# Batched float32 matmul: late stores gated by half of the last batch but one, and the last quarter of the first x loaded in sixteen transfers of eight partitions

## The chip, the cores and the metric

The kernel runs on one core of one Trainium2 chip. The metric is the device time in microseconds (us) of one execution. The time before was 517.37 us, the median of three runs (517.19 to 517.54).

"The profile" is a page of one profiled execution, and "the trace" is the record behind it: every instruction, every DMA packet with queue, size, start and duration, and every completion signal. PE is the matmul engine, SyncE and GpSimd (SP and POOL in the profile) issue DMA transfers here, and sixteen DMA engines carry them.

## The reference

```python
def setup_inputs():
    batch, m, k, n = 32, 512, 1024, 768
    return {
        "x": np.random.randn(batch, m, k).astype(np.float32),
        "weight": np.random.randn(batch, k, n).astype(np.float32),
    }

def reference(x, weight):
    return np.matmul(x, weight).astype(np.float32)
```

The program reads 64 MiB of x and 96 MiB of weights and writes 48 MiB, with no reuse between batches.

## The kernel before

x and weights are loaded by GpSimd, which casts them to bf16 on the way. Only the x of batch 0 comes in float32 through SyncE, because that queue starts sooner (its first issue begins at 0.74 us, GpSimd's at 1.23). Stores go through GpSimd too, up to the last four; those go through SyncE at the end. Loads run three to four batches ahead of the arithmetic.

```python
CHUNKED = {B - 4: (4, 4), B - 3: (4, 4), B - 2: (4, 4), B - 1: (4, 2, 2)}
AHEAD = 3
LATE = 4
...
def load_x(b):
    xs[b] = x_pool.tile([P, MT, K], BF16, name="x_sb")
    nc.gpsimd.dma_start(out=xs[b], in_=x_view[b])
...
def transpose_first(mt):
    xT = xT_pool.tile([P, JT, P, 2], BF16, name="xT")
    for h in range(2):
        pt = tpsum.tile([P, JT, P], F32, name="pt")
        for i in range(JT):
            nc.tensor.transpose(pt[:, i, :], x_first[:, mt, JT * h + i::KT], ident)
        ...
...
x_first = first_pool.tile([P, MT, K], F32)      # 128 partitions, 16 KB each
nc.sync.dma_start(x_first, x_view[0])
load_w(0)
...
for b in range(B):
    if b + AHEAD + 1 < B:
        load_x(b + AHEAD + 1)
    if b + AHEAD < B:
        load_w(b + AHEAD)
    if 0 < b <= B - LATE:
        nc.gpsimd.dma_start(out=out_view[b - 1], in_=outs[b - 1])
    if b == B - 1:
        for late in (B - 2, *range(B - LATE, B - 2)):
            nc.sync.dma_start(out_view[late], outs[late])
    ...
                if last and mt % 2 == 1:
                    pair = mt // 2
                    evacuate(b, pair, pms[pair])
                    if b == B - 1:
                        cols = slice(pair * N2, (pair + 1) * N2)
                        nc.sync.dma_start(out_view[b, :, cols], outs[b][:, cols])
```

The store of batch 30 (B - 2) is the first of the late ones on SyncE, and the others queue behind it, so it is the gate of them all.

## Time and profile before

| what | value | view |
|---|---|---|
| time, median of three runs | 517.37 us | times |
| span of the profiled run | 515.6 us | page |
| data moved | 218.1 MB, 423 GB/s | page, DMA queues |
| chain of waits | DMA 89%, PE 7% | page, chain |
| PE may start on the last two batches / PE ends | 481.2 / 507.3 us | chain, by time |
| last weights piece: first to last of its 16 signals | 490.82 to 495.91 us | completion signals |
| last store, last signal | 514.26 us | completion signals |

Lines of the page of the kernel before. The PE and DMA lines are tenths of busy time in 40 slices of the span. The q lines are DMA queues with packets, MB and their share of the sixteen engines' time. The DMA/PE line is the chain that ended last, and the last line is the group of transposes of x_first (busy us, mean ns, then the idle time ahead of them and what ended it).

```profile
span 515.6 us, 5976 instructions
...
PE   0999898698797888869978799797798877999793
...
DMA  8999999999999999999999999999999999999996
...
q0 software_dynamic: 13824, 126.88, 96.8%
q1 hardware_dynamic: 864, 8.39, 4.0%
q8 instruction: 20, 0.33, 0.2%
...
HBM read 167.77 MB, written 50.33 MB: 423 GB/s over the span
...
DMA 89%; PE 7%; issue 1%; POOL 1%; DVE 0%; ACT 0%; POOLq 0%
...
L82 PE MATMUL pt<-ident,x_first 128*128 128x128 f32 x32 | 6.0, 350 | 12.2 <-DMA x_first<-in_x_dram 12.2
```

The DMA engines are busy in every slice but the last, and the chain that sets the end is nearly all DMA. q0 is the queue of the GpSimd transfers, q1 that of the SyncE ones.

The windows view of the end of the kernel before (per stretch: us from the start, then its length, busy us of PE, PE's weight loads, DVE, ACT and POOL, the granted clock, the DMA busy share, GB/s):

```profile
490.00:494.00 4.00, 4.00 (x26) 2.44 (x25) 0.69 (x1) 1.76 (x3) 0.00 (x0) 1.00 1.07 320
494.00:496.00 2.00, 1.70 (x13) 1.35 (x12) 1.69 (x3) 0.59 (x1) 0.00 (x0) 1.00 0.72 286
496.00:504.00 8.00, 8.00 (x54) 5.34 (x53) 1.67 (x3) 0.00 (x0) 0.00 (x0) 1.00 1.01 424
504.00:508.00 4.00, 3.27 (x21) 1.73 (x18) 1.38 (x2) 2.30 (x4) 0.00 (x0) 1.00 0.96 404
508.00:512.00 4.00, 0.00 (x0) 0.00 (x0) 0.00 (x0) 0.00 (x0) 0.00 (x0) 1.00 0.85 350
512.00:514.00 2.00, 0.00 (x0) 0.00 (x0) 0.00 (x0) 0.00 (x0) 0.00 (x0) 0.64 0.14 58
```

There is one dip, at 494 to 496 us, where the share is 0.72: engines that have finished their loads wait for the gate. From 508 us on the engines drop out one after another.

The reason is that the engines are not equally far along. Each transfer leaves sixteen completion signals. These are the landing offsets of the last weights piece, in us after the first signal, for the kernel before (worked out from the trace):

```
first 490.82, last 495.91:
0.0 0.1 0.1 0.3 0.3 0.9 1.4 2.0 2.5 2.6 2.6 2.6 2.7 4.2 4.2 5.1
```

The trace does not number the engines. But packets on one engine follow each other, so following each packet's end to the next one's start puts nearly all of them on sixteen chains. Queue 8 carries 20 blocks of instructions of 16 KB. They fall on the same eight chains in a cycle, two or three on each, and on the other eight never. The Trainium skill, "Runtime: NRT & Kernel Launch", Instruction fetch mechanics, says that instructions are refilled in 16 KiB blocks over DMA queues of their own; this trace agrees (20 packets of 16 KB), and shows on which engines the cost falls.

### The profile page before, as it was taken

To read this page: it belongs to the slowest core of one execution; us is meant where nothing else is said; L and a number is where in the kernel's file an instruction comes from. 1 tells how busy PE (TensorE), PEld (TensorE's weight loads), DVE (VectorE), ACT (ScalarE), POOL (GpSimd) and SP (SyncE) were. 2 spreads that over 40 slices of the span, in tenths; PEclk is the share of its full clock that TensorE was granted. 3 is DMA by queue.
4 is the path that set the end of the run, shared out by engine and by line. 5 is a ranking of instruction groups with operands and counts; after the bars stand their busy time and mean duration, and the time that the engine had idled before them with its cause. 6 is when DMAs were issued, how large, how long until landed. Compare 5 with 4: busy or idle time off the path is not lost.

```text
span 515.6 us, 5976 instructions
## 1 busy us (share of the span) xinstructions
PE 429.0 (83%) x2576; PEld 279.2 (54%) x2576; DVE 129.8 (25%) x196; ACT 76.3 (15%) x129; POOL 51.9 (10%) x102
## 2 busy tenths in 40 slices
PE   0999898698797888869978799797798877999793
PEld 0666565465464555546645466464465545665461
DVE  0433232213232312221223232122222313232231
ACT  0011111111011111111111111011110111111011
POOL 3011100011011010100101001100111010111000
PEclk9999899989799988988989999799998989899898
DMA  8999999999999999999999999999999999999996
GB/s 255 218 218 211 218 271 275 256 237 276 277 275 269 231 273 276 274 274 245 251 278 276 274 260 242 272 274 275 269 243 263 277 273 275 247 248 272 274 368 285
DMA packets 14713, 135.64 MB, mean 263 GB/s; under 512 B 1632, under 2 KB 1632, under 8 KB 3040
## 3 DMA queue, kind: packets, MB, share of 16 engines
q0 software_dynamic: 13824, 126.88, 96.8%
q1 hardware_dynamic: 864, 8.39, 4.0%
q8 instruction: 20, 0.33, 0.2%
q14 instruction: 5, 0.04, 0.0%
HBM read 167.77 MB, written 50.33 MB: 423 GB/s over the span
## 4 chain that ended last, share of the span: by engine, by line
DMA 89%; PE 7%; issue 1%; POOL 1%; DVE 0%; ACT 0%; POOLq 0%
DMA w_sb<-in_weight_dram 39%; DMA x_sb<-in_x_dram 25%; DMA out_dram<-out_sb 25%; PE pm L100 7%; PE pt L69 1%; POOL w_sb L61 0%; POOL x_sb L55 0%; ACT out_sb L113 0%; DVE out_sb L112 0%; DVE xT L71 0%; POOL ident masks.py:199 0%; POOL ident masks.py:197 0%; POOLq L132 0%; POOLq L61 0%; POOLq masks.py:199 0%
## 5 line engine op out<-in xcount | busy, mean ns | idle before, releaser
L100 PE MATMUL pm<-w_sb,xT 128*128 128x256 bf16 (+1 forms) x2048 | 374.1, 342 | 66.1 <-DMA w_sb<-in_weight_dram 63.7
L100 PEld LDWEIGHTS <-xT 128*128 128x128 bf16 x2048 | 207.0, 102 | 208.2 <-issue 77.0
L71 DVE COPY xT<-pt 128x1024 bf16<-128x1024 bf16 x124 | 82.9, 689 | 230.6 <-PE pt L69 230.6
L111 ACT COPY out_sb<-pm 128x512 f32<-128x512 f32 x64 | 37.5, 587 | 293.3 <-PE pm L100 293.3
L69 PEld LDWEIGHTS pt<-ident,x_sb 128*128 128x128 f32 x496 | 72.7, 206 | 6.6 <-issue 1.9
L112 DVE COPY out_sb<-pm 128x512 f32<-128x512 f32 x64 | 44.0, 687 | 128.1 <-PE pm L100 128.1
L69 PE MATMUL pt<-ident,x_sb 128*128 128x128 f32 x496 | 75.3, 285 | 0.0
L113 ACT COPY out_sb<-pm 128x512 f32<-128x512 f32 x64 | 37.5, 587 | 137.5 <-PE pm L100 137.4
L55 POOL DMA_DIRECT2D x_sb<-in_x_dram x31 | 16.5, 534 | 176.5 <-DMA w_sb<-in_weight_dram 150.9
L61 POOL DMA_DIRECT2D w_sb<-in_weight_dram x37 | 19.8, 536 | 126.0 <-DMA out_dram<-out_sb 62.8
L132 POOL DMA_DIRECT2D out_dram<-out_sb x28 | 15.1, 538 | 119.0 <-DMA x_sb<-in_x_dram 57.3
L82 PE MATMUL pt<-ident,x_first 128*128 128x128 f32 x32 | 6.0, 350 | 12.2 <-DMA x_first<-in_x_dram 12.2
L82 PEld LDWEIGHTS pt<-ident,x_first 128*128 128x128 f32 x32 | 5.0, 204 | 12.8 <-issue 12.2
L83 DVE CAST xT<-pt 128x512 bf16<-128x512 f32 x8 | 5.6, 728 | 19.2 <-PE pt L82 19.0
L111 ACT ACT_TABLE_LOAD x1 | 1.3, 1283 | 0.7 <-PEq L180 0.7
masks.py:199 POOL TENSOR_SCALAR_AFFINE_SELECT ident<-ident 128x128 f32<-128x128 f32 x1 | 0.3, 289 | 0.1
masks.py:197 POOL MEMSET ident<- 128x128 f32 x1 | 0.2, 224 | 0.0
L180 POOL MEMSET const-float32-0.0<- 128x1 f32 x1 | 0.1, 99 | 0.2 <-issue 0.2
L180 POOL MEMSET const-bfloat16-1.0<- 128x1 bf16 x1 | 0.1, 102 | 0.0
L180 POOL MEMSET const-uint8-127<- 128x1 uint8 x1 | 0.1, 102 | 0.0
L180 POOL MEMSET const-float32-1.0<- 128x1 f32 x1 | 0.1, 99 | 0.0
## 6 DMA issues: line engine op xcount, KB each, us to landing
w_sb<-in_weight_dram POOLq DMA_DIRECT2D x28, 1536.0 KB, 43.2
out_dram<-out_sb POOLq DMA_DIRECT2D x28, 1536.0 KB, 42.0
x_sb<-in_x_dram POOLq DMA_DIRECT2D x31, 1024.0 KB, 39.6
w_sb<-in_weight_dram POOLq DMA_DIRECT2D x7, 768.0 KB, 31.4
out_dram<-out_sb SPq DMA_DIRECT2D x3, 1536.0 KB, 11.4
x_first<-in_x_dram SPq DMA_DIRECT2D x1, 2048.0 KB, 11.3
out_dram<-out_sb SPq DMA_DIRECT2D x2, 768.0 KB, 6.1
w_sb<-in_weight_dram POOLq DMA_DIRECT2D x2, 384.0 KB, 27.5
```

Source lines behind the costliest of these rows:

```text
L55: nc.gpsimd.dma_start(out=xs[b], in_=x_view[b])
L61: nc.gpsimd.dma_start(out=ws[b][:, at:at + n, :], in_=w_view[b, :, at:at + n, :])
L69: nc.tensor.transpose(pt[:, j, :], pairs[:, mt, j::JT], ident)
L71: nc.vector.tensor_copy(xT.rearrange("p j m r -> p (j m r)"), pt.bitcast(BF16).rearrange("p j m -> p (j m)"))
L82: nc.tensor.transpose(pt[:, i, :], x_first[:, mt, JT * h + i::KT], ident)
L83: nc.vector.tensor_copy(xT[:, 2 * h:2 * h + 2].rearrange("p j m r -> p j r m"), pt.rearrange("p (j r) m -> p j r m", r=2),)
L100: nc.tensor.matmul(pm[bank][:, at:at + size], xT[:, ko // 2, :, ko % 2], ws[b][:, ko, off:off + size], start=(ko == 0 and not (together an ...
L111: nc.scalar.copy(o[:, 0:512], pm[0])
L112: nc.vector.tensor_copy(o[:, 512:1024], pm[1])
L113: nc.scalar.copy(o[:, 1024:N2], pm[2])
L132: nc.gpsimd.dma_start(out=out_view[b - 1], in_=outs[b - 1])
L180: nc = _bacc.Bacc("TRN2", target_bir_lowering=False, num_devices=1)
```

## The change

There are two parts. At the start, the last quarter of x_first (partitions x 4 KB) is taken out of the one big transfer and sent in sixteen transfers of eight partitions, meant to load eight DMA engines and to spare the eight others. At the end, the store of batch 30 is cut in halves by columns: the first half, which is evacuated earlier, is the new gate, and the second half goes last. The last piece only gives the slices a common name.

```diff
-        nc.sync.dma_start(x_first, x_view[0])
+        nc.sync.dma_start(x_first[:, :MT - 1], x_view[0, :, :MT - 1])
         load_w(0)
+
+        for half in range(0, P, 32):
+            for at in range(half, half + 4):
+                few = slice(at, half + 32, 4)
+                nc.sync.dma_start(x_first[few, MT - 1], x_view[0, few, MT - 1])
 ...
             if b == B - 1:
-                for late in (B - 2, *range(B - LATE, B - 2)):
+                halves = [slice(pair * N2, (pair + 1) * N2) for pair in range(2)]
+                nc.sync.dma_start(out_view[b - 1, :, halves[0]], outs[b - 1][:, halves[0]])
+                for late in range(B - LATE, B - 2):
                     nc.sync.dma_start(out_view[late], outs[late])
+                nc.sync.dma_start(out_view[b - 1, :, halves[1]], outs[b - 1][:, halves[1]])
 ...
                         if b == B - 1:
-                            cols = slice(pair * N2, (pair + 1) * N2)
-                            nc.sync.dma_start(out_view[b, :, cols], outs[b][:, cols])
+                            nc.sync.dma_start(out_view[b, :, halves[pair]], outs[b][:, halves[pair]])
```

## The prediction

> **What bounds the kernel.** The DMA engines. The page's slices show their mean busy share near 9 tenths throughout; the chain of waits is 89% DMA, PE 7%; HBM moves 218 MB at 423 GB/s. So two things count: the work of each of the sixteen engines, and idle time of the engine that ends last.
>
> **The engines are not equally loaded.** Each transfer leaves sixteen completion signals in the trace. First to last, they are 0.6 us apart for the first weights, 2.3 us at 110 us, 4.0 us at 230 us, 5.1 us from 430 us on. Following packets end to start, I can put them on sixteen engines: the 20 instruction blocks of 16 KB (queue 8, 0.93 us each) fall on the same eight engines in turn, two or three each (1.9 to 2.8 us); the other eight carry none. The Trainium skill, "Runtime: NRT & Kernel Launch", Instruction fetch mechanics, says instructions are refilled in 16 KiB blocks; the trace agrees.
>
> At the end, twelve engines finish the last store by 511.9 us, four at 513.2 to 514.3. Fast ones idle 0.9 to 2.0 us around 494 to 496 (the windows view: DMA share 0.72), because stores on the SyncE queue wait for the whole of batch 30 (495.0); the slowest never idles: its late stores land 3.66 us apart, eight packets of 0.46 us each.
>
> **What the change does.**
> 1. x_first: three quarters over sixteen engines, the last 512 KB on eight. The Trainium skill, "DMA: Bandwidth & Descriptors", How many engines (k), says a SyncE transfer of eight partitions uses the lowest-numbered eight. They get 16 rows of 4 KB in place of 8, the others none. A 16 KB row takes 0.624 us, so 4 KB about 0.156: +1.25 us for eight engines, -1.25 us for eight. I assume that the relieved eight are those with instruction blocks; the order of their first packets leans that way, no proof.
> 2. Sixteen small issues, each taking turns with weight packets of 0.93 us: the last quarter should land at 20 to 24 us; its first use was at 22.8. PE may stall up to 2 us in batch 0; free, since transfers are queued some 40 us ahead.
> 3. Gate: the first half of batch 30 is evacuated at 492.5 us, 2.5 us before the whole. That fills idle time of engines which do not end last: about 0 alone. Rows of 6 KB cost 0.236 us against 0.461 for 12 KB, nothing lost.
>
> **On the critical path.** The slowest engine loses 1.25 us at the start and never idles, so its later landings move up by 1.25 us. Weights that release PE at 481.2 us come earlier too, so PE's end (507.3 us) moves up; from there a last half store needs about 3.5 us, so PE does not bind. 517.37 - 1.25 = 516.1 us. Range 515.4 to 517.2. Faster by over 2%: 0.01; within 2%: 0.98; slower: 0.01.
>
> **What would show it.** Spread of the signals late in the run down from 5.1 to about 2.6 us, with an early spread up to about 2.5 us; span 514.4 us; the dip at 494 to 496 us gone; hardware-queue packets of 4 KB near 0.16 us; the last quarter landing at 20 to 24 us, PE idle at most 2 us in batch 0.
>
> **What would make it wrong.** If the instruction blocks sit on the lowest eight, the skew grows to 7.6 us and the time rises to about 518.6 us. If 4 KB packets cost much more than 0.16 us, the filled engines become the last. If batch 0 stalls for long, the queue could run dry. If the earlier stores hold up the weights of batch 31 on the slow engine, PE ends later and gain is lost.

## The result, and the profile after

The changed kernel took 517.19 us (median of six runs, 516.93 to 518.73), the kernel before in the same rounds 517.45 us (six runs, 516.89 to 517.77). The ratio is 1.0000, with a 95% interval of 0.9987 to 1.0014. Here and below a ratio is the mean time of one kernel's fast runs over the mean of the other's of the same rounds, so it is not quite the ratio of the medians quoted. The forecast gain of 1.25 us is not there: the interval allows at most 0.7 us. In the profile the span is the same too.

Lines of the page after, answering to those of before:

```profile
span 515.6 us, 5998 instructions
...
PE   0039999999999889769978799788798796998793
...
DMA  8999999999999999999999999999999999999996
...
q1 hardware_dynamic: 1264, 8.39, 4.1%
q8 instruction: 20, 0.33, 0.2%
...
DMA 70%; PE 25%; DVE 2%; issue 1%; ACT 0%; POOLq 0%
...
L82 PE MATMUL pt<-ident,x_first 128*128 128x128 f32 x32 | 6.0, 349 | 34.1 <-DMA x_first<-in_x_dram 34.1
```

PE starts batch 0 at 34.1 us instead of 12.2 us, then works without gaps for about ten slices until it has caught up. That is also why the chain now counts 25% for PE: while PE catches up, the chain can be followed through it. The DMA line is the same.

The timeline of the first 36 us after (start, length, engine, line, operation, count):

```profile
0.74 0.39 SPq L117 DMA_DIRECT2D x_first<-in_x_dram  x1
1.19 20.85 SPq L123 DMA_DIRECT2D x_first<-in_x_dram  x16
...
34.05 2.39 PE L82 MATMUL pt<-ident,x_first 128*128 128x128 f32 x9 [34.05 <-DMA x_first<-in_x_dram]
```

The waits view of SyncE's queue after (what its line waited for: us in total, times, longest us):

```profile
SPq L123 <- DMA x_first<-in_x_dram: 10.3, 9, 4.1
```

The sixteen issues take from 1.2 to 22 us: each is 0.62 us long, and nine of them wait 10.3 us in all for earlier transfers. The last of their signals arrive at 33.2 to 34.0 us, and only then does PE start, although its first transposes read the three quarters that had landed by 10.1 us.

The windows view of the end after:

```profile
490.00:494.00 4.00, 4.00 (x28) 2.44 (x26) 0.69 (x1) 1.76 (x3) 0.00 (x0) 1.00 1.07 324
494.00:496.00 2.00, 1.70 (x14) 1.36 (x12) 1.82 (x3) 0.59 (x1) 0.00 (x0) 1.00 0.99 392
496.00:504.00 8.00, 8.00 (x54) 5.30 (x52) 1.54 (x3) 0.00 (x0) 0.00 (x0) 1.00 1.02 430
504.00:508.00 4.00, 3.14 (x19) 1.66 (x17) 1.38 (x2) 2.30 (x4) 0.00 (x0) 1.00 0.81 339
508.00:512.00 4.00, 0.00 (x0) 0.00 (x0) 0.00 (x0) 0.00 (x0) 0.00 (x0) 0.65 0.84 343
512.00:514.00 2.00, 0.00 (x0) 0.00 (x0) 0.00 (x0) 0.00 (x0) 0.00 (x0) 0.50 0.10 43
```

The dip at 494 to 496 us is filled (0.72 to 0.99), and comes back at 504 to 508 us (0.96 to 0.81): the fast engines finish the earlier stores sooner and then wait for PE's last halves. The chain by time says that PE's end hardly moved. Before, then after (start, length, what):

```profile
450.05 31.16 DMA w_sb<-in_weight_dram
...
481.35 2.26 PE pm L100 x8
...
507.31 0.59 ACT out_sb L113
```

```profile
450.58 30.50 DMA w_sb<-in_weight_dram
...
481.21 2.08 PE pm L100 x8
...
507.18 0.59 ACT out_sb L113
```

The weights that release PE land at 481.08 us instead of 481.21, and the last evacuation starts 0.13 us earlier. The forecast said 1.25.

What about the engines? The last weights piece now lands from 489.90 to 495.78 us, so the spread of its signals is 5.9 us, not the forecast 2.6. The next table adds up the time of each chain up to its 700th data packet on the software queue, the same amount of bulk work for every engine. "hw" is the time of data packets on the SyncE queue, "blocks" that of instruction blocks, "stalled" the time by which packets of the software queue took longer than the median for their size. The rest (start, bulk packets, overlap) is nearly the same for all, 458.4 to 459.6 us on the chains that end last.

```
                                        reached at        hw         blocks       stalled
before  no blocks (seven of eight)      465.4 to 466.8    5.4-6.2    0            0.4 to 1.5
        two blocks (six)                468.0 to 468.3    5.8-6.0    1.9          1.0 to 1.4
        three blocks                    470.53            5.96       2.68         3.00
        three blocks                    469.60            5.69       2.68         2.38
after   no blocks, relieved (two)       464.5 to 464.6    4.1-4.5    0            0.4 to 0.6
        two blocks, relieved (six)      466.7 to 467.1    4.6-5.1    1.9          0.7 to 0.9
        no blocks, filled (five)        466.9 to 467.3    7.1-8.0    0            0.4 to 0.6
        three blocks, filled            470.39            7.77       2.68         0.99
        three blocks, filled            470.18            7.93       2.68         1.09
```

(One chain of each kernel is left out: it also carries two 8 KB instruction packets of another queue; it is at 467.0 before and at 468.4 after. The links between packets are inferred. A second linking holds each engine to its eight data packets of every large transfer. It gives the same points and blocks, but for the last two chains after it gives 7.39 and 7.57 us of hw and 1.39 and 1.09 of stalls. So the points are firm, and the split between hw and stalls is good to about 0.4 us.)

Two things stand out. Six of the eight engines with blocks were relieved, and gained 1.3 us; but the two with three blocks before the end, which end last, are among the filled eight. And although those two now carry about 2 us more (1.5 to 1.9 in the second linking), the later of them comes no later than before (470.39 against 470.53): their stalls are 1.3 to 2.0 us shorter (1.3 to 1.6 in the second linking).

### The profile page after: what moved, and what is told of

Same layout as the page of the kernel before. It is cut to its first block, busy times and chain, and to the rows that moved or that the text cites. A ratio compares the mean times of both kernels' runs of the same rounds, so it can differ in the third digit from the quotient of the medians.

```text
span 515.6 us, 5998 instructions
## 1 busy us (share of the span) xinstructions
PE 422.0 (82%) x2576; PEld 276.9 (54%) x2576; DVE 129.8 (25%) x196; ACT 76.3 (15%) x129; POOL 51.9 (10%) x102
## 4 chain that ended last, share of the span: by engine, by line
DMA 70%; PE 25%; DVE 2%; issue 1%; ACT 0%; POOLq 0%
DMA w_sb<-in_weight_dram 31%; DMA out_dram<-out_sb 24%; PE pm L100 22%; DMA x_sb<-in_x_dram 8%; DMA x_first<-in_x_dram 6%; PE pt L69 2%; DVE xT L71 1%; PE pt L82 1%; DVE out_sb L112 1%; ACT out_sb L113 0%; POOLq L61 0%; POOLq L137 0%; POOLq L55 0%
## 5 line engine op out<-in xcount | busy, mean ns | idle before, releaser
L100 PE MATMUL pm<-w_sb,xT 128*128 128x256 bf16 (+1 forms) x2048 | 367.1, 337 | 51.1 <-DMA w_sb<-in_weight_dram 47.4
L100 PEld LDWEIGHTS <-xT 128*128 128x128 bf16 x2048 | 204.5, 101 | 188.8 <-issue 54.6
L82 PE MATMUL pt<-ident,x_first 128*128 128x128 f32 x32 | 6.0, 349 | 34.1 <-DMA x_first<-in_x_dram 34.1
```

Of the source, the lines that this page charges most:

```text
L100: nc.tensor.matmul(pm[bank][:, at:at + size], xT[:, ko // 2, :, ko % 2], ws[b][:, ko, off:off + size], start=(ko == 0 and not (together an ...
```

## The experiments

The theory after the first look at the trace was: the filled eight include two of the block engines, so the engine that ends last gets more work and not less; something else hides the extra. The rivals: the gate or the split undoes a gain of the other; PE's late start costs what the relief gives; the placing of the blocks is drawn anew in each run, so that the two traces can't be compared. The quoted expectations name these theories in their own words or by letters.

### Half of the change: the gate alone

```diff
             if b == B - 1:
-                for late in (B - 2, *range(B - LATE, B - 2)):
+                halves = [slice(pair * N2, (pair + 1) * N2) for pair in range(2)]
+                nc.sync.dma_start(out_view[b - 1, :, halves[0]], outs[b - 1][:, halves[0]])
+                for late in range(B - LATE, B - 2):
                     nc.sync.dma_start(out_view[late], outs[late])
+                nc.sync.dma_start(out_view[b - 1, :, halves[1]], outs[b - 1][:, halves[1]])
```

> Kernel before with the gate alone: x_first as one transfer, late stores as in the change. My theory (the engine that ends last never idles near 494 us): 517.4 us, within 0.3 us of before; the idle of the fast engines moves from 494 to 496 us to about 504 to 508 us. Rival (the gate costs time and hides a gain of the split): 518.3 us or more. A second rival (the idle near 494 us counts): 516.8 us or less.

Measured: 517.36 us (516.86 to 517.71) against 517.25 before (eleven runs), ratio 0.9997 (0.9985 to 1.0009). The windows view of this run:

```profile
494.00:496.00 2.00, 1.65 (x12) 1.26 (x12) 1.91 (x3) 0.58 (x1) 0.00 (x0) 1.00 0.97 389
...
504.00:508.00 4.00, 2.89 (x18) 1.48 (x16) 1.38 (x2) 2.30 (x4) 0.00 (x0) 1.00 0.83 349
```

The gate does what was wanted of it, fills the dip (0.72 to 0.97) and moves it (0.96 to 0.83), and is worth nothing that these runs can show (the interval goes from 0.8 us gained to 0.5 lost).

### The other half: the split alone

```diff
-        nc.sync.dma_start(x_first, x_view[0])
+        nc.sync.dma_start(x_first[:, :MT - 1], x_view[0, :, :MT - 1])
         load_w(0)
+        for half in range(0, P, 32):
+            for at in range(half, half + 4):
+                few = slice(at, half + 32, 4)
+                nc.sync.dma_start(x_first[few, MT - 1], x_view[0, few, MT - 1])
```

> Kernel before with the split of x_first alone. My theory (six of the eight relieved engines carry instruction blocks, but the two that take the first and second block are among the filled eight and become the last): within 0.4 us of before, PE starting near 34 us, spread of the completion signals near 5.9 us late in the run. Rival (the gate hid the gain of the split): 516.2 us.

Measured: 517.40 us (517.19 to 519.00), ratio 1.0009 (0.9993 to 1.0024). The two chains with three blocks are filled here too (7.82 and 7.66 us of hw) and end the count at 470.18 and 470.19 us with stalls of 1.09 and 1.15, as in the changed kernel. So neither half hides a gain of the other; the missing gain is in the split.

### Load added to eight engines, and to six partitions' worth

Two probes add work to the kernel before that nobody uses: sixteen loads of 3 KB rows into a scratch tile, on eight partitions or on six.

```diff
         load_w(0)
+        scratch = scratch_pool.tile([P, N], F32)
+        for half in range(0, P, 32):
+            for at in range(half, half + 4):
+                few = slice(at, half + 32, 4)      # extra6: half + 24
+                nc.sync.dma_start(scratch[few], x_view[0, few, MT - 1, :N])
```

> Kernel before, plus sixteen loads of 8 partitions of 3 KB that nothing reads, so the lowest eight engines get 16 packets of about 0.134 us = 2.1 us more, the others none. My theory (the slowest engine is among the lowest eight and never idles): 519.5 us, 2.1 us over before. Rival (all engines with instruction blocks are in the highest eight, and the others have about 2.6 us to spare): within 0.3 us of before. Wrong in no output.

Measured: 517.76 us (517.41 to 519.71), ratio 1.0012 (0.9997 to 1.0027). Sixteen packets of 0.134 us are 2.1 us on each of eight engines; the end moved by 0.5 us in the medians, and in the trace the last store lands at 515.05 instead of 514.26 us. The chain that ends last had 7.92 us of hw instead of 5.96, and 1.78 us of stalls instead of 3.00. This is a miss for a plain sum rule (2.1 expected), and the first sign that stalls give way when load is added.

> As extra8, but of 6 partitions, so the load falls on the lowest six engines alone. If the two loaded-and-filled engines are numbers 6 and 7 (blocks go to eight consecutive engines from 6 on): within 0.3 us of before, since the lowest six have 3 to 5 us to spare. If one of them is among the lowest six: 519.5 us as in extra8.

Measured: 517.45 us (516.97 to 519.76), ratio 1.0006 (0.9989 to 1.0023): no cost to be seen. In its trace one of the six filled engines carries blocks, where two of the eight did; for that case 519.5 us was expected, so this is a miss too. The kernel differs here in a second way: its cycle starts elsewhere, so that this engine carries two blocks and not three, and stands at 469.96 us (second linking), before the 470.53 of the last engine in the kernel before. Together with the relieved and filled chains of the changed kernel, this narrows down which engines are which: of the lowest eight, two carry blocks, of the lowest six one. That the filled engines are the lowest-numbered is what the Trainium skill says in "DMA: Bandwidth & Descriptors", How many engines (k), for transfers issued by SyncE; the trace has no numbers to confirm it, but agrees that each small transfer falls on the same eight (or six) chains, up to a packet or so that the following misplaces.

### Are blocks and stalls drawn anew in each run?

The two kernels were run again, unedited, for one more trace each.

> The kernel before, unchanged, profiled once more. Two of the eight engines that carry instruction blocks show shorter block packets (0.892 us against 0.94 to 0.97), and took blocks 0 and 1 (so three each) in the profiles of before, of the change and of the split alone, blocks 2 and 3 in those of the gate alone and of extra8, blocks 4 and 5 in that of extra6. Theory A (where the cycle starts is a state of the chip, not of the program): another start in this profile than in the first one is possible, and the engine that ends last differs with it. Theory B (the program fixes it): again blocks 0 and 1. Theory C on the stalls: the burst of stalled packets at 66 to 68 us (5.8 us over all engines) is there again.

> The changed kernel, unchanged, profiled once more. Theory A: another start of the cycle is possible; if the two engines with 0.892 us blocks then carry two blocks each and not three, the spread of the signals late in the run is about 4.7 us and the time about 516.3 us. Theory B: again blocks 0 and 1, spread 5.8 us, about 517.2 us. No burst of stalls at 66 to 68 us (under 1 us).

Measured: 517.37 and 517.38 us, one run each, state unknown. In both second traces the cycle of the blocks starts on the same two engines as in the first traces, so the program fixes it and not the run. The stalls are a property of the program too, at least roughly. Stalled time summed over all software packets (worked out from the packet records). Here only packets more than some 40 ns over the median count; the table of chains above counts every excess, which makes 19.0 us in the kernel before and 11.4 in the changed one:

```
                    whole run   60 to 110 us
before              12.7 us     8.1
before, again        9.6        5.0
gate alone          12.5        8.1
gate alone, again    9.3        5.1
after                5.2        0.7
after, again         4.6        0.2
split alone          5.3        0.4
```

Each trace of the kernel before has a burst of stalled packets at 66 to 68 us, of 5.8 us in the first and 2.2 in the second; the changed kernel has 0.3 us or less there. The burst is spread over the engines, so it is at most 0.84 us of the last engine's 3.00. The two probes with even load below have no burst either, though nothing is skewed in them: 0.0 us there with load added, 0.2 with a quarter left out.

### PE's late start taken away

```diff
-        x_first = first_pool.tile([P, MT, K], F32)
-        nc.sync.dma_start(x_first[:, :MT - 1], x_view[0, :, :MT - 1])
+        x_first = first_pool.tile([P, MT - 1, K], F32)
+        x_last = last_pool.tile([P, K], F32)
+        nc.sync.dma_start(x_first, x_view[0, :, :MT - 1])
 ...
-                nc.sync.dma_start(x_first[few, MT - 1], x_view[0, few, MT - 1])
+                nc.sync.dma_start(x_last[few], x_view[0, few, MT - 1])
```

(The last quarter's transposes read x_last.)

> The changed kernel with the last quarter of the first x in a tile of its own, so that the transposes of the first three quarters do not wait for it. PE then starts near 11 to 15 us in place of 34 us. My theory (the late start of PE is made up by about 190 us and costs nothing): time as of the change, within 0.3 us. Rival (the late start hides a gain): about 516.1 us.

Measured: 517.18 us (516.88 to 517.24) against 517.03 before (nine runs), ratio 0.9999 (0.9986 to 1.0013). The timeline of this run:

```profile
1.20 20.25 SPq L126 DMA_DIRECT2D x_last<-in_x_dram  x16
...
10.31 3.89 PE L84 MATMUL pt<-ident,x_first 128*128 128x128 f32 x16 [10.31 <-DMA x_first<-in_x_dram]
```

PE starts at 10.3 us instead of 34.1, and the time is the same. So the late start was caused by sharing one tile, whose transposes waited for all seventeen transfers into it, and it cost nothing, because the loads were queued far ahead and PE had slack to catch up. That rival falls.

### The gate alone once more

> The gate alone once more, with five rounds beside the others of this call: 517.3 us, within 0.3 us of before, as in the first call. It shows how far the same kernel differs from call to call, and whether the start of the cycle (blocks 2 and 3 in its first profile) is the same.

This is the same kernel as the gate alone, run again on another chip. Measured: 517.16 us (516.55 to 518.19), ratio 1.0003 (0.9991 to 1.0016). The two engines that carry blocks 0 and 1 in the kernel before carry blocks 2 and 3 here, in both of its traces. So a program keeps the start of its cycle from run to run and chip to chip, and another program may start elsewhere. Why is open.

### Does load at the start come out at the end?

```diff
 (extra16)
+        for _ in range(2):
+            nc.sync.dma_start(scratch, x_view[0, :, MT - 1, :N])
```

```diff
 (skip_quarter; wrong output on purpose: the third quarter is used twice)
-        x_first = first_pool.tile([P, MT, K], F32)
-        nc.sync.dma_start(x_first, x_view[0])
+        x_first = first_pool.tile([P, MT - 1, K], F32)
+        nc.sync.dma_start(x_first, x_view[0, :, :MT - 1])
```

> Kernel before plus two loads of 128 rows of 3 KB that nothing reads: every one of the sixteen engines gets 16 packets of about 0.134 us = 2.1 us more (extra8 gave them to eight engines and cost 0.5 to 0.8 us). My theory (the engine that ends last is never idle, so what is put on it at the start comes out at the end): 519.3 us, 2.1 us over before. Rival (the end is set by PE and the last evacuations, DMA has slack): within 0.4 us of before.

> Kernel before without the load of the last quarter of the first x (the third quarter is used twice: wrong output in one batch, on purpose). Every engine is relieved of 8 rows of 4 KB, 1.25 us, as the change does for eight of them. My theory: 516.0 us, 1.25 us under before: what the change would gain if its relief reached all engines with instruction blocks at no cost to any of them. Rival (PE or something else takes over within that): less than 0.6 us gained.

Measured: with 2.1 us more on all sixteen engines 519.22 us (518.85 to 519.52) against 517.29 before (nine runs), ratio 1.0035 (1.0022 to 1.0047), so 1.9 us more. Without the last quarter 516.21 us (515.55 to 516.57), ratio 0.9972 (0.9958 to 0.9986), so 1.1 us less, where the forecast for such a relief was 1.25. (Its output is wrong on purpose, with a relative error of 0.125.) The first lines of their pages, in this order:

```profile
span 517.1 us, 5979 instructions
```

```profile
span 514.8 us, 5976 instructions
```

So the step "what an engine carries at 10 us comes out at 514 us" holds when all sixteen get it. In the change, the relief did not reach the two engines that end last; that these did not end later either does not follow from this step.

### The same idea on the four lowest engines

If none of the four lowest engines carries blocks, filling only these relieves all eight block engines. Half of the last quarter goes over all sixteen, the other half in sixteen transfers of four partitions.

```diff
 (against the changed kernel; x_last has a tile of its own, the gate is kept)
-        for half in range(0, P, 32):
-            for at in range(half, half + 4):
-                few = slice(at, half + 32, 4)
-                nc.sync.dma_start(x_first[few, MT - 1], x_view[0, few, MT - 1])
+        nc.sync.dma_start(x_last[:P // 2], x_view[0, :P // 2, MT - 1])
+        for at in range(P // 2, P, 4):
+            nc.sync.dma_start(x_last[at:at + 4], x_view[0, at:at + 4, MT - 1])
```

> The changed kernel with a milder shift: of the last quarter, 64 rows over all sixteen engines and 64 rows by sixteen transfers of 4 partitions, in a tile of its own. Lowest four engines: 12 rows more than before (about 2.0 us), the other twelve: 4 rows less (0.64 us). If no engine among the lowest four carries instruction blocks, the last engine ends 0.6 us earlier: 516.7 us. If one of the two that carry blocks and are filled in the change is among them: 518.5 to 519.4 us, and it ends last.

Measured: 516.34 us (five runs, 516.29 to 516.45) against 517.29, ratio 0.9979 (0.9966 to 0.9991), and correct. That is 1.0 us, or 0.2%, faster than the kernel before in the same rounds; the changed kernel was not among them, but it only equalled the kernel before in its own. The first line of its page and its instruction queue:

```profile
span 514.5 us, 6000 instructions
...
q8 instruction: 20, 0.33, 0.2%
```

The 20 blocks are still there; only the engines differ. The chains of this run, as in the table above:

```
four    no blocks (four)                464.8 to 465.7    4.4-5.9    0            0.4 to 0.7
        two blocks (six)                467.0 to 467.7    5.2-5.6    1.8-1.9      0.7 to 1.0
        three blocks                    468.87            5.66       2.92         1.10
        three blocks                    469.04            5.17       2.88         1.39
        filled, no blocks (four)        467.6 to 468.9    7.3-8.4    0            0.4 to 0.7
```

No filled chain carries a 16 KB block, and the latest filled one (468.87 us) is level with the most loaded block engines. How much of the gain is relief? The gate alone is the fair partner: it has the same gate, and its blocks start at the same place. Its last chain stood at 470.20 us, with hw 6.09, blocks 2.88 and stalls 2.08. Against it, four has 0.92 us less hw, 0.69 us less stalls and 0.45 us more of the rest, together 1.16 us less. The second linking puts the same 1.16 down to 0.48 of hw, 0.62 of stalls and 0.06 of the rest. So a relief of about 0.5 us is there, near the 0.64 that was forecast, but stalls make up more than half of the net gain.

### A milder fill of eight, and no skew at all

```diff
 (eight_mild, against four)
-        for at in range(P // 2, P, 4):
-            nc.sync.dma_start(x_last[at:at + 4], x_view[0, at:at + 4, MT - 1])
+        for at in range(P // 2, P, 8):
+            nc.sync.dma_start(x_last[at:at + 8], x_view[0, at:at + 8, MT - 1])
```

```diff
 (even, against four)
-        nc.sync.dma_start(x_last[:P // 2], x_view[0, :P // 2, MT - 1])
-        for at in range(P // 2, P, 4):
-            nc.sync.dma_start(x_last[at:at + 4], x_view[0, at:at + 4, MT - 1])
+        nc.sync.dma_start(x_last, x_view[0, :, MT - 1])
```

> As four, but the second 64 rows by eight transfers of 8 partitions: the lowest eight engines have 4 rows more than before (about 0.7 us), the others 4 less (0.64 us). Sum rule (what an engine carries, blocks and stalls included, sets its end): the two lowest engines with blocks get 0.7 to 0.9 us more and lose 1.5 to 2 us of stalls, so they end 0.7 to 1 us earlier than before: about 516.5 us, nearly as four. Rival (four is faster because its filled engines carry no blocks): 517.2 us or more.

> As own_tile, but the last quarter as one transfer of 128 partitions: split, no skew between engines, load per engine about as before (+0.2 us). If the skew between two groups of engines is what removes the burst of stalls at 66 to 68 us: the burst is back (5 to 8 us in all from 60 to 110 us) and the time is that of before, 517.3 us. If the split as such removes it: under 1 us of stalls there, and 1 us or more faster than before.

Measured: eight_mild 516.88 us (516.57 to 517.38) against 517.15 before (eleven runs), ratio 0.9993 (0.9981 to 1.0006). That is between what the two theories expected and decides nothing. Its two filled chains with three blocks carry 7.02 us of hw each, stall for 2.14 and 1.56 us (about 1.1 was expected) and stand at 470.48 and 469.94 us, as in the kernel before. even took 517.23 us (516.66 to 518.81), ratio 1.0008 (0.9995 to 1.0021). It has no skew, and a stalled time of 9.6 us, like the other kernels without skew; but the burst at 66 to 68 us is gone (1.8 us of stalls from 60 to 110 us), and stalls sit elsewhere, at 84 and 138 us. So the burst is not what the skew takes away, and the expected story of the stalls is not clean on either side.

## Why the prediction was wrong

**The step that failed.** The prediction put it so: "I assume that the relieved eight are those with instruction blocks". Six of the eight block engines were relieved, and two were filled, and these two are the ones which in this program carry a third block before the end and finish last. The prediction knew this as a risk and gave 518.6 us for it, on the assumption that all blocks sit on the lowest eight. With two there, the slowest engine is just as much filled, so the term "-1.25 us on the engine that ends last" had the wrong sign: that engine carried about 1.8 us more (hw 5.96 to 7.8 us; 1.5 in the second linking), and by the sum should have ended that much later.

**Why it did not even lose.** On that engine the stalls fell from 3.00 to 0.99 us, which takes 2.0 us away: +1.8 of hw, -2.0 of stalls, +0.1 of the rest give 470.39 instead of 470.53 us (+1.5, -1.6 and 0.0 in the second linking). The second trace of the changed kernel, the split alone and the kernel with the own tile all show much the same stalls on these two chains, 0.9 to 1.2 us (1.0 to 1.3 in the second linking). That this exchange happened is measured. Why is open, so the runs show why there was no gain, and not why there was no loss. Summed over the engines, stalls were 9.3 to 12.7 us in seven traces of five kernels without skew (12.7 and 9.6, 12.5 and 9.3, 9.6, 11.1, 11.5), and 4.6 to 7.8 us in six traces of five kernels in which the skew replaced part of x_first (5.2 and 4.6, 5.3, 5.1, 6.4, 7.8). But the two probes that skewed by adding load had 13.5 and 8.8. A skew alone therefore doesn't explain them, and an account by the burst was refuted by the kernel without skew.

**The terms that were mis-sized.** A row of 4 KB was put at 0.156 us, a quarter of 0.624; it took 0.172, and the remaining 12 KB took 0.473, not 0.468. By these medians the filled engines carry 16 x 0.172 + 8 x 0.473 = 6.5 us in place of 8 x 0.624 = 5.0, so 1.5 us more and not 1.25. The chains that end last show 1.8 to 2.2 more (1.5 to 1.9 in the second linking), as single packets took longer than the median. The relief was about right: 4.6 to 5.1 us after 5.8 to 6.0 on six engines.

**The landing and PE's start.** The last quarter was to land at 20 to 24 us and PE to idle at most 2 us. It landed at 33.2 to 34.0 us, and PE idled to 34.1. Two steps failed. First, the sixteen do not land one per 0.93 us packet: their signals on a chain are about 1.5 us apart, from 10.7 to 33.3 us. Most steps are 1.98 or 1.38 us. That fits two turns per transfer, one for the data and one for its completion packet, each alternating with a weight packet or an x packet: 2 x 0.926 + 0.172 = 2.02 and 2 x 0.625 + 0.172 = 1.42. The Trainium skill, "DMA: Bandwidth & Descriptors", Queues, rings and completion order, says that an engine goes round-robin between its queues packet by packet; the steps agree with that, if a completion packet counts as a turn. The trace shows that it does: on the chains of the second linking, 127 of the 128 packets of 4 KB are followed by one software packet before their own completion packet. Second, the prediction overlooked that transposes of the early quarters wait for every transfer into the tile. Its conclusion, that such a stall is free, was right nevertheless (own tile: 10.3 us instead of 34.1, same time).

**What was right.** The kernel is bound by DMA, and by the engine that ends last. The 20 blocks fall on eight engines. The gate fills the dip and is worth about 0. PE does not bind at the end. And the rule that work at the start comes out at the end was right where all sixteen engines got the same: 1.9 us more for 2.1, 1.1 us less for the quarter of 1.25 taken out. With block-free engines alone filled, 1.0 us was gained where 0.6 was forecast, the excess by shorter stalls; with eight engines loaded, 0.5 us of 2.1 came out.

**What stays open:** what the stalls are and why they give way on the filled engines; and what in a program fixes at which engine its cycle of blocks starts.

## What to carry to other kernels

When a kernel is bound by sixteen DMA engines, its time is that of the engine that ends last, so first find out from completion signals and packet chains which engine that is and what it carries (here instruction blocks), and only then shift work; a probe that adds work to a known set of engines tells membership more safely than an order of first packets. A rule of sums that holds with load on all engines (1.9 of 2.1 us) need not hold with load on some (0.5 of 2.1 us on eight), so test it in both ways. Give a piece that lands late a tile of its own if early work reads the rest, even where, as here, that turned out to be free.

## What the Trainium skill lacked or had wrong

- "Runtime: NRT & Kernel Launch", Instruction fetch mechanics, calls the cost of crossing a 16 KiB block "one DMA tail-bump, mostly hidden". For the sequencer that may be so, no run here shows it; for a kernel bound by DMA it is not hidden: each of 20 blocks takes 0.94 us of one DMA engine, and most data packets right after one take about 0.2 us longer than their median. In the kernel before, engines with two blocks reach the same point 2.4 us later in the median than those without (468.11 against 465.68 us), and the two with three blocks are the last (469.60 and 470.53 us).
- No page says that these blocks go to eight of the sixteen engines in a fixed cycle, that a program keeps the start of this cycle in repeated runs (two traces each of three kernels), or that another program may start elsewhere (the low two block engines took blocks 0 and 1 in the kernel before, 2 and 3 with the gate alone).
- "DMA: Bandwidth & Descriptors", How many engines (k), gives the engines of a small transfer, and the traces agree as far as they can (the same eight, six or four chains each time). It does not say that two of the lowest eight engines, one of the lowest six and, in one trace, none of the lowest four carry instruction blocks.
- No page gives a size or a tested cause for the stalled packets: 4.6 to 13.5 us in a run, summed over the engines, with a burst of 5.8 us in 22 packets at 66.4 to 68.2 us in the kernel before.
- For "DMA: Bandwidth & Descriptors", the runs give per-row times of one engine: rows of 16, 12, 4 and 3 KB on the SyncE queue take 0.624, 0.473, 0.172 and 0.134 us, so not quite in proportion to size.
